# The last row tile of a hybrid attention block: order of three products and the way its normalization is put together

## Chip, cores, metric

One core of a Trainium2 chip runs the whole program. The metric is device time in microseconds (us); lower is better. Engines: TensorE (PE in the profile), VectorE (DVE), ScalarE (ACT), GpSimd (POOL), SyncE (SP).

## The reference

One encoder block for x of 1024 tokens × 1024 channels, float32. Two attention groups (a neighbourhood attention over a 16 × 64 grid and a windowed attention with a sink) give `mixed`, each multiplied by SiLU of its gate. What the change touches is the end:

```
y = mixed @ w_out                       # 1024 x 1024 times 1024 x 1024
x = layer_norm(alpha * x + y) * gain + bias
```

with mean and deviation taken over the 1024 channels of each token.

## The kernel before

Up to about 390 us the kernel projects the input and runs the attention, with an order of work planned in advance (steps, due times and costs per engine). The edit lies behind that, in `final()`, where the order is written out by hand: per engine, instructions run in the order of the lines, and engines wait for one another on semaphores.

**The output product** is done in 2 × 2 blocks with shared partial products in the manner of Strassen, over the first half of the sum, and with plain products over the rest. The loop in `final()` goes over t = 0..3. Pass t finishes two row tiles of 128 tokens: row tile t and row tile 4 + t. Their columns come in two halves of 512: half 0 and half 1. `prod` (L1168) issues the matmuls of one named product, each term three matmuls (high and low float16 parts), 512 columns each. A PSUM bank holds a running sum to which several products are added in turn, and `add` (L1210) lets VectorE add the bank's present content, times a constant, to the row tile `xr` (L1213):

- q1: goes into half 0 of row tile t; in pass 3 its bank is `b[3]`
- q6: added into the same bank; the sum goes into half 1 of row tile t
- q5: its own bank; into half 1 of row tiles t and 4 + t
- q7: added into `b[t]` on top of q6; into half 1 of row tile 4 + t
- d: own bank; half 1 of row tile 4 + t
- p4: added into `b[t]`; half 0 of row tile 4 + t
- q2: half 0 of row tile t (18 matmuls in pass 3)
- q3: half 1 of row tile t; in pass 3 in pieces of 256, 128 and 128 columns

Since q7 is added onto the bank that holds q6, q7 may only start once VectorE has read the bank. With `whole=True` `add` also issues the statistics of the piece (`bn_stats`, L1219; for row tile 3 in pieces of 128). In pass 3 the order on TensorE before the change is q5, q6, q2 (first 6 matmuls), q7, d, p4, q2 (other 12), q3 in three pieces.

**The normalization** of most row tiles is `begin` and `finish`: VectorE puts the statistics together (`bn_aggr`, L1223), ScalarE takes the root (L1225), ScalarE applies scale and shift to the row tile (L1284), GpSimd multiplies by gain and adds bias (L1286, L1287), SyncE sends two transfers of 256 KB (L1288). `norm(7)`, ahead of row tile 3's end, lets VectorE do half of the columns (L1277, L1281).

Row tile 3 comes last. `norm_ahead` (L1238) lets GpSimd multiply its first WP = 256 columns (`HP`) by gain ahead of time. `norm_last` (L1240) then puts bias for these columns into a PSUM bank through the identity (L1243), runs 30 matmuls whose result isn't used (L1246), takes mean (`mv`) and deviation (`sd`), and adds two more matmuls: a diagonal matrix of 1/deviation times x·gain (`dr`, L1251, L1253) and one of -mean/deviation times gain (`dn`, L1252, L1254). ScalarE copies the bank out (L1256). VectorE scales the other columns in two pieces, `H0` (256) and `H1` (512): first (x - mean)·gain (L1248, L1255), then times 1/deviation plus bias (L1258). SyncE sends the two pieces (L1259), ScalarE's queue the first 256 columns (L1260).

Of the kernel before, what the change touches and what calls it, by code (L numbers as in the profile page):

```python
# [7 lines left out]
F32 = mybir.dt.float32  # L8
# [4 lines left out]
AF = mybir.ActivationFunctionType  # L13
ALU = mybir.AluOpType
# [41 lines left out]
WORK = {"act": 0.55, "dve": 0.63, "pool": 1.2}  # L56
STEP = (1.88, 1.5, 1.2)
ROOM = {"act": 0.35, "dve": 0.5, "pool": 0.0}
WP = 256
BWIN = (0, 256, 624, 880)  # L60
VE = HD + 1
ROPE_PERM = list(range(0, 16)) + list(range(32, 48)) + list(range(16, 32)) + list(range(48, 64))
# [3 lines left out]
def hybrid_block(ctx, tc, xT, x, wt, wv, wo, bias, sink, gain, lbias, cos, sin, bmask, out):  # L66
    nc = tc.nc
# [10 lines left out]
    def bank(tag):  # L78
        bufs = {"pj": 2, "s": 4, "t": 2}[tag]
        return (ps1 if bufs == 1 else ps2).tile([128, 512], F32, tag=tag, name=f"ps_{tag}", bufs=bufs)  # L80
# [6 lines left out]
    def big_tile(name, shape=(128, 2, 512), dt=F32R):  # L87
        n = taken[0]
        taken[0] += 1
        tag = "big" if n < 8 or 16 <= n < 24 or n >= 32 + NS else "big2"  # L90
        return big.tile(list(shape), dt, tag=tag, name=name)

    xh, xl, x16h, x16l = {}, {}, {}, {}
    for half in range(2):
        for k in range(KT):
            t = big_tile(f"x{half}{k}", dt=F32 if half else F32R)
# [3 lines left out]
    def zslot(name, tag="z"):  # L100
        return zp.tile([128, S], F32, tag=tag, name=name, bufs=3 if tag == "z" else 1)


    identf = const.tile([128, 128], F32, name="identf")
# [797 lines left out]
    def quad(q):  # L902
        g, p, j, t = units[4 * q]
        return g, p, j, t // 4
# [263 lines left out]
    def prod(name, t, ps, es=None, c=(0, 512)):  # L1168
        o, w = c
        cs = slice(o, o + w)  # L1170
        terms = TERMS[name]
        fresh = name in ("q1", "q2", "q5", "d") or c != (0, 512)
        for e in range(len(terms)) if es is None else es:
            a, b, i = terms[e]
            need(*done.get((a, i), ()), *done.get((b, i), ()))
            (ah, al), (bh, bl) = part[a, i], part[b, i]
            for n, (lh, rh) in enumerate(((ah, bh), (ah, bl), (al, bh))):
                nc.tensor.matmul(ps[:, cs], lh[:, 128 * t:128 * t + 128], rh[:, cs],  # L1178
                                 start=(fresh and e == 0 and n == 0), stop=(e == len(terms) - 1 and n == 2), skip_group_check=True)
                yield  # L1180
# [14 lines left out]
    def final():  # L1195
        actx.close()
        fp = ctx.enter_context(tc.tile_pool(name="fp", bufs=2, reuse_waits="tile"))
# [9 lines left out]
        def x_scale(t):  # L1207
            nc.scalar.activation(xrs[t], xrs[t], AF.Copy, scale=ALPHA)

        def add(t, a, ps, c=(0, 512), whole=False):  # L1210
            o, w = c
            xv = xrs[t][:, 512 * a + o:512 * a + o + w]
            nc.vector.scalar_tensor_tensor(xv, ps[:, o:o + w], yc, xv, op0=ALU.mult, op1=ALU.add)  # L1213
            if whole:
                if t not in stats:
                    stats[t] = fp.tile([128, 8, 6], F32, name=f"stats{t}", bufs=1)
                b = 128 if t == 3 else 512
                for i in range(w // b):
                    nc.vector.bn_stats(stats[t][:, (512 * a + o) // b + i, :], xv[:, b * i:b * i + b])  # L1219

        def row_stats(t):
            mv = fp.tile([128, 2], F32, tag="mv", name="mv")
            nc.vector.bn_aggr(mv, stats[t][:, :8 if t == 3 else 2, :])  # L1223
            sd = fp.tile([128, 1], F32, tag="sd", name="sd")
            nc.scalar.activation(sd, mv[:, 1:2], AF.Sqrt, bias=eps)  # L1225
            return mv, sd

        def row_scale(mv, sd, on_dve=True):
            rstd = fp.tile([128, 1], F32, tag="rstd", name="rstd")
            nc.vector.reciprocal(rstd, sd)  # L1230
            nmr = fp.tile([128, 1], F32, tag="nmr", name="nmr")
            (nc.vector if on_dve else nc.gpsimd).tensor_scalar(nmr, mv[:, 0:1], rstd, -1.0, op0=ALU.mult, op1=ALU.mult)  # L1232
            return rstd, nmr

        HP, H0, H1 = slice(0, WP), slice(WP, WP + 256), slice(WP + 256, 1024)

        def norm_ahead(t):
            nc.gpsimd.tensor_mul(xrs[t][:, HP], xrs[t][:, HP], gb[:, HP])  # L1238

        def norm_last(t):  # L1240
            ts = slice(128 * t, 128 * t + 128)
            xr = xrs[t]
            nc.tensor.matmul(pn[:, :WP], identf, bb[:, HP], start=True, stop=False)  # L1243
            busy = bank("s")
            for _ in range(30):
                nc.tensor.matmul(busy[:, :128], warm, warm, start=True, stop=True)  # L1246
            mv, sd = row_stats(t)
            nc.vector.scalar_tensor_tensor(xr[:, H0], xr[:, H0], mv[:, 0:1], gb[:, H0], op0=ALU.subtract, op1=ALU.mult)  # L1248
            rstd, nmr = row_scale(mv, sd)
            dr, dn = (fp.tile([128, 128], F32, name=n, bufs=1) for n in ("dr", "dn"))  # L1250
            nc.scalar.activation(dr, identf, AF.Copy, scale=rstd)  # L1251
            nc.scalar.activation(dn, identf, AF.Copy, scale=nmr)  # L1252
            nc.tensor.matmul(pn[:, :WP], dr, xr[:, HP], start=False, stop=False)  # L1253
            nc.tensor.matmul(pn[:, :WP], dn, gb[:, HP], start=False, stop=True)  # L1254
            nc.vector.scalar_tensor_tensor(xr[:, H1], xr[:, H1], mv[:, 0:1], gb[:, H1], op0=ALU.subtract, op1=ALU.mult)  # L1255
            nc.scalar.copy(xr[:, HP], pn[:, :WP])  # L1256
            for h in (H0, H1):
                nc.vector.scalar_tensor_tensor(xr[:, h], xr[:, h], rstd, bb[:, h], op0=ALU.mult, op1=ALU.add)  # L1258
                nc.sync.dma_start(out[ts, h], xr[:, h])  # L1259
            nc.scalar.dma_start(out[ts, HP], xr[:, HP])  # L1260
# [3 lines left out]
        def begin(t):  # L1264
            begun.append((t, *row_stats(t)))

        def finish():
            while begun:
                norm(*begun.pop())
# [23 lines left out]
        a, b = ([obank.get((name, t)) for t in range(4)] for name in ("q2", "q1"))  # L1293
        add(0, 0, b[0])
        m_last()
        gb, bb = zslot("gb"), zslot("bb")
# [8 lines left out]
        def run(name, t, ps, *args):  # L1305
            list(prod(name, t, ps, *args))
            return ps

        c01 = [run("q5", t, bank("t")) for t in range(2)]
        for t in range(4):  # L1310
            cb = c01[t] if t < 2 else run("q5", t, bank("s"))
            if t == 0:
                run("q2", 0, a[0], (5,))
                add(0, 0, a[0], whole=True)
                run("q2", 1, a[1], (5,))
            run("q6", t, b[t])
            if t > 0:
                add(4 + t, 1, cb)
            add(t, 1, b[t])
            if t == 3:  # L1320
                add(t, 1, cb)
            finish()
            if t == 0:
                add(4, 1, cb)
                add(1, 0, b[1])
                add(1, 0, a[1], whole=True)
            if t == 1:
                add(2, 0, b[2])
                run("q2", 2, a[2], (5,))
                add(2, 0, a[2], whole=True)  # L1330
            for n in ((5, 2), (6, 3), (7,), ())[t]:
                x_scale(n)
            if t < 3:
                d = run("d", t, bank("pj"))
                run("q7", t, b[t])
            else:
                a[3] = run("q2", 3, bank("pj"), (0, 1))
                run("q7", t, b[t])
                add(7, 1, b[3])
                d = run("d", t, bank("pj"))  # L1340
            add(4 + t, 1, d, whole=t == 3)
            if t < 3:
                add(4 + t, 1, b[t], whole=True)
            if t == 2:
                b[3] = run("q1", 3, bank("s"))
                add(3, 0, b[3])
            if t < 3:
                run("q3", t, cb)
                add(t, 1, cb, whole=True)
                begin(t)  # L1350
            run("p4", t, b[t])
            add(4 + t, 0, b[t], whole=True)
            if t == 3:
                norm(7)
            else:
                finish()
                begin(4 + t)
        add(3, 0, run("q2", 3, a[3], range(2, 6)), whole=True)
        norm_ahead(3)
        cuts = [((0, 256), bank("t")), ((256, 128), None), ((384, 128), None)]  # L1360
        pn = bank("t")
        for c, ps in cuts:
            ps = ps or bank("pj" if c[0] == 256 else "s")
            add(3, 1, run("q3", 3, ps, None, c), c, whole=True)
        norm_last(3)

    def m_last():
# [14 lines left out]
    for i in range(-LD, NU + LO):  # L1382
# [5 lines left out]
        per, h = divmod(i, 16)  # L1388
# [3 lines left out]
        if i in SCAN_LD:  # L1392
            n, b = divmod(NSCAN + SCAN_LD.index(i), 4)
# [9 lines left out]
        if i in B_LD:  # L1403
            n = B_LD.index(i)
# [50 lines left out]
        if 0 <= q < NU // 4:  # L1455
            g, p, j, h = quad(q)
# [93 lines left out]
```

## Time and profile before

| | |
|---|---|
| median of 3 runs | 442.7 us (443.14, 442.70, 441.31) |
| the profiled execution | 441.67 us |
| its span in the trace | 439.9 us |
| TensorE busy | 433.5 us (99%) |
| VectorE, ScalarE, GpSimd busy | 335.0, 314.2, 279.4 us |
| granted TensorE clock | 0.999 |

The execution is the device's time for the run; the span is what the trace covers, from the first instruction to the last. Starts in the rows are us from the beginning of the span. A group `128x512 f32<-128x512 f32 x2` gives partitions × elements of output and input, and the count. In merged rows the length runs to the modelled end of the last matmul, so neighbouring TensorE rows overlap a little.

### The profile page before, as it was taken

Reading aid. Unit: us, or ns where it says so; the run is one execution under the profiler, and the core shown is the slowest. Engines: PE = TensorE matmul, PEld = TensorE weight load, DVE = VectorE, ACT = ScalarE, POOL = GpSimd, SP = SyncE. Lnnn points to the kernel's source line nnn. Section 1 sums busy time; section 2 is a strip of 40 time slices with the busy share of each in tenths; the row PEclk is TensorE's granted clock in tenths of the full one; section 3 lists DMA queues with packets and bytes.
Section 4 is the critical chain, followed back from the end, with each engine's and each line's share of the span. In section 5 each row is a group of like instructions: output and inputs, shape, how many; then the busy total and the mean of one; then the engine's idle time right before and its main releaser. Section 6 shows DMA issues by size and latency. Waiting matters only on the chain.

```text
span 439.9 us, 9401 instructions
## 1 busy us (share of the span) xinstructions
PE 433.5 (99%) x3235; PEld 253.7 (58%) x3235; DVE 335.0 (76%) x820; ACT 314.2 (71%) x662; POOL 279.4 (64%) x299
## 2 busy tenths in 40 slices
PE   9999999999999999999999999999999999999995
PEld 8997754444445555565555565655556555444454
DVE  5978967775978798889788977878778855575556
ACT  5849789767698889798988979788788763341221
POOL 0110074577439558779998799797989871067683
PEclk9999999999999999999999999999999999999999
DMA  8922569995329998996859999989799959711113
GB/s 273 406 82 60 140 235 332 260 302 166 101 67 196 187 192 172 212 165 122 194 106 214 218 210 195 221 184 181 147 203 214 169 114 372 288 48 75 70 73 120
DMA packets 128815, 80.12 MB, mean 182 GB/s; under 512 B 97280, under 2 KB 106368, under 8 KB 128768
## 3 DMA queue, kind: packets, MB, share of 16 engines
q1 hardware_dynamic: 128624, 79.40, 73.9%
q8 instruction: 25, 0.41, 0.4%
q14 instruction: 22, 0.18, 0.1%
q10 hardware_dynamic: 144, 0.13, 0.1%
HBM read 48.01 MB, written 8.42 MB: 128 GB/s over the span
## 4 chain that ended last, share of the span: by engine, by line
PE 97%; DVE 2%; ACT 0%; issue 0%; DVEq 0%; ACTq 0%
PE ps_pj L430 49%; PE ps_s L1178 9%; PE ps_t L925 7%; PE ps_s L537 6%; PE ps_pj L1178 4%; PE ps_s L860 4%; PE ps_s L861 4%; PE ps_pj L537 3%; PE ps_t L537 3%; PE ps_t L1178 2%; PE ps_t L948 2%; PE ps_t L463 1%; DVE stats L1219 1%; DVE xr L1213 1%; DVE xr L1281 0%
## 5 line engine op out<-in xcount | busy, mean ns | idle before, releaser
L430 PE MATMUL ps_pj<-xf,wh 128*128 128x512 f16 x672 | 201.5, 379 | 0.0
L430 PE MATMUL ps_pj<-xf,wl 128*128 128x512 f16 x336 | 127.5, 379 | 0.0
L430 PEld LDWEIGHTS <-wh 128*128 128x128 f16 x672 | 63.7, 98 | 59.8
L885 ACT ACTIVATE ps_s<-sn,nm 128x385 f32<-128x385 f32 (+3 forms) x128 | 71.0, 554 | 30.2 <-DVE nm L870 29.7
L896 DVE SCALAR_TENSOR_TENSOR split<-ps_s,split 128x384 f16<-128x384 f32 (+1 forms) x128 | 66.8, 522 | 17.8 <-ACT split L895 16.3
L245 POOL TENSOR_SCALAR wr<-wr,wsc 128x512 f32<-128x512 f32 x32 | 22.9, 717 | 65.2 <-ACT wh L240 59.9
L895 ACT ACTIVATE split<-ps_s 128x384 f16<-128x384 f32 (+1 forms) x128 | 58.1, 454 | 1.6
L430 PEld LDWEIGHTS <-wl 128*128 128x128 f16 x336 | 32.9, 98 | 38.1
L870 DVE CUSTOM_DVE_ANT_0 sn<-ps_s,bias,sg 128x368 f32<-128x368 f32 (+1 forms) x64 | 36.2, 566 | 13.8 <-PE ps_s L861 13.2
L870 DVE CUSTOM_DVE_ANT_0 sn<-ps_s,bm,nsk 128x384 f32<-128x384 f32 (+1 forms) x64 | 40.8, 638 | 6.5 <-PE ps_s L861 6.1
L246 POOL TENSOR_TENSOR wl<-wr,wh 128x512 f16<-128x512 f32 x32 | 40.3, 1261 | 2.7
L860 PE MATMUL ps_s<-ks,qs 128*128 128x384 f16 (+2 forms) x128 | 39.7, 310 | 0.0
L861 PE MATMUL ps_s<-ks,qs 128*128 128x384 f16 (+2 forms) x128 | 39.7, 310 | 0.0
L925 PEld LDWEIGHTS <-tr 128*128 128x128 f16 (+1 forms) x1056 | 36.3, 98 | 2.4
L1178 PEld LDWEIGHTS <-A 128*128 128x128 f16 x216 | 20.2, 98 | 20.7
L347 POOL COPY ks<-ks 64x512 f16<-64x512 f16 x40 | 25.9, 647 | 4.6 <-ACT ks L298 2.0
L1213 DVE SCALAR_TENSOR_TENSOR xr<-ps_s,yc,xr 128x512 f32<-128x512 f32 (+1 forms) x22 | 16.0, 727 | 14.8 <-PE ps_s L1178 14.0
L1284 ACT ACTIVATE xr<-xr,nmr,rstd 128x1024 f32<-128x1024 f32 x6 | 7.4, 1240 | 27.0 <-POOL nmr L1232 27.0
L1178 PEld LDWEIGHTS <-m 128*128 128x128 f16 x144 | 13.9, 98 | 15.8
L537 PEld LDWEIGHTS <-xf 128*128 128x128 f16 x192 | 18.6, 98 | 7.2
L240 ACT ACTIVATE wh<-wr,wsc 128x512 f16<-128x512 f32 x32 | 22.7, 710 | 0.0
L1286 POOL TENSOR_TENSOR xr<-xr,gb 128x512 f32<-128x512 f32 x13 | 16.8, 1291 | 8.3 <-ACT xr L1284 8.1
(216 smaller groups left out, 897.7 us busy)
## 6 DMA issues: line engine op xcount, KB each, us to landing
wr<-in_wt SPq DMA_DIRECT2D x32, 256.0 KB, 3.6
ws<-in_wt SPq DMA_DIRECT2D x15, 512.0 KB, 6.8
wor<-in_wo SPq DMA_DIRECT2D x20, 256.0 KB, 3.7
xr<-in_x SPq DMA_DIRECT2D x8, 512.0 KB, 10.5
out<-xr SPq DMA_DIRECT2D x15, 256.0 KB, 2.0
wob<-in_wo SPq DMA_DIRECT2D x14, 256.0 KB, 3.8
bias<-in_bias SPq DMA_DIRECT2D x8, 440.0 KB, 4.5
wvraw<-in_wv SPq DMA_DIRECT2D x9, 320.0 KB, 5.3
```

What stands on the lines that cost most here:

```text
L246: nc.gpsimd.tensor_sub(l, raw, h)
L347: nc.gpsimd.tensor_copy(place(t, o, half, col), place(t, a, half, col))
L430: nc.tensor.matmul(ps, a[:, k % 4, :], mv, start=(k == 0 and i == 0), stop=(k == KT - 1 and i == 2))
L537: nc.tensor.matmul(ps[:, :320], lh[:, ts], rh[:, cs], start=(k == ko[0] and i == 0), stop=(k == ko[-1] and i == 2))
L860: nc.tensor.matmul(ps[:, :n], q, sl[0], start=True, stop=False)
L861: nc.tensor.matmul(ps[:, :n], q, sl[1], start=False, stop=True)
L870: nc.vector.tensor_tensor_reduce(sn[:, :n], ps[:, :n], bias_t, sg[:, c:c + 1], init, op0=ALU.add, op1=ALU.min, accum_out=nm)
L885: nc.scalar.activation(pt[:, :m], sn[:, :m], AF.Exp, bias=nm, scale=-1.0, accum_out=acc)
L895: nc.scalar.activation(hl[:, :m, 0, :], src, AF.Copy, scale=PSCALE)
L896: nc.vector.scalar_tensor_tensor(hl[:, :m, 1, :], src, PSCALE, hl[:, :m, 0, :], op0=ALU.mult, op1=ALU.subtract)
L925: nc.tensor.matmul(ps[:, w * m:w * m + e], a, b_, start=(i == 0), stop=(i == len(mms) - 1))
L1178: nc.tensor.matmul(ps[:, cs], lh[:, 128 * t:128 * t + 128], rh[:, cs], start=(fresh and e == 0 and n == 0), stop=(e == len(terms) - 1 and ...
```

## The change

Three things, all in the last pass and behind it:

1. In pass 3 the order becomes q6, q5, q7, d, p4, q2 (all 18 matmuls in one go), q3. q6's sum is read by VectorE's first add, then come the two adds of q5.
2. WP becomes 384: the first 384 columns of row tile 3 go through the bank, `H0` is columns 384 to 640 and `H1` columns 640 to 1024 (384 of them).
3. In `norm_last` the bank gets three matmuls: the identity times x·gain, a diagonal matrix `dm` of -mean (made by GpSimd) times gain, and a diagonal matrix `ds` of the deviation (made by ScalarE) times bias. ScalarE multiplies by 1/deviation while it copies the bank out. The unused matmuls become 20 and stand ahead of the identity's matmul. `H1` is scaled and sent ahead of `H0`.

```
-WP = 256
+WP = 384
...
-            nc.tensor.matmul(pn[:, :WP], identf, bb[:, HP], start=True, stop=False)
             busy = bank("s")
-            for _ in range(30):
+            for _ in range(20):
                 nc.tensor.matmul(busy[:, :128], warm, warm, start=True, stop=True)
+            nc.tensor.matmul(pn[:, :WP], identf, xr[:, HP], start=True, stop=False)
             mv, sd = row_stats(t)
+            rstd = fp.tile([128, 1], F32, tag="rstd", name="rstd")
+            dm, ds = (fp.tile([128, 128], F32, name=n, bufs=1) for n in ("dm", "ds"))
+            nc.gpsimd.tensor_scalar(dm, identf, mv[:, 0:1], -1.0, op0=ALU.mult, op1=ALU.mult)
+            nc.scalar.activation(ds, identf, AF.Copy, scale=sd)
+            nc.tensor.matmul(pn[:, :WP], dm, gb[:, HP], start=False, stop=False)
+            nc.tensor.matmul(pn[:, :WP], ds, bb[:, HP], start=False, stop=True)
+            nc.vector.scalar_tensor_tensor(xr[:, H1], xr[:, H1], mv[:, 0:1], gb[:, H1], op0=ALU.subtract, op1=ALU.mult)
+            nc.vector.reciprocal(rstd, sd)
             nc.vector.scalar_tensor_tensor(xr[:, H0], xr[:, H0], mv[:, 0:1], gb[:, H0], op0=ALU.subtract, op1=ALU.mult)
-            rstd, nmr = row_scale(mv, sd)
-            dr, dn = (fp.tile([128, 128], F32, name=n, bufs=1) for n in ("dr", "dn"))
-            nc.scalar.activation(dr, identf, AF.Copy, scale=rstd)
-            nc.scalar.activation(dn, identf, AF.Copy, scale=nmr)
-            nc.tensor.matmul(pn[:, :WP], dr, xr[:, HP], start=False, stop=False)
-            nc.tensor.matmul(pn[:, :WP], dn, gb[:, HP], start=False, stop=True)
-            nc.vector.scalar_tensor_tensor(xr[:, H1], xr[:, H1], mv[:, 0:1], gb[:, H1], op0=ALU.subtract, op1=ALU.mult)
-            nc.scalar.copy(xr[:, HP], pn[:, :WP])
-            for h in (H0, H1):
+            nc.scalar.activation(xr[:, HP], pn[:, :WP], AF.Copy, scale=rstd)
+            for h in (H1, H0):
                 nc.vector.scalar_tensor_tensor(xr[:, h], xr[:, h], rstd, bb[:, h], op0=ALU.mult, op1=ALU.add)
                 nc.sync.dma_start(out[ts, h], xr[:, h])
             nc.scalar.dma_start(out[ts, HP], xr[:, HP])
...
         for t in range(4):
-            cb = c01[t] if t < 2 else run("q5", t, bank("s"))
+            cb = c01[t] if t < 2 else run("q5", t, bank("s")) if t == 2 else None
...
             run("q6", t, b[t])
+            if t == 3:
+                add(t, 1, b[t])
+                cb = run("q5", t, bank("s"))
             if t > 0:
                 add(4 + t, 1, cb)
-            add(t, 1, b[t])
-            if t == 3:
-                add(t, 1, cb)
+            add(t, 1, cb if t == 3 else b[t])
             finish()
...
             else:
-                a[3] = run("q2", 3, bank("pj"), (0, 1))
                 run("q7", t, b[t])
...
-        add(3, 0, run("q2", 3, a[3], range(2, 6)), whole=True)
+        add(3, 0, run("q2", 3, bank("pj")), whole=True)
```

## The prediction

> **What bounds the kernel now.** I read the page first, then the chain of work that ended last, then the timelines of the last 25 us by engine. The page:
>
> ```profile
> span 439.9 us, 9401 instructions
> ```
> ```profile
> PE 97%; DVE 2%; ACT 0%; issue 0%; DVEq 0%; ACTq 0%
> ```
>
> TensorE carries 97% of the chain. The edit starts at the loop pass t = 3, so only the end of the program can move. There the chain of waits changes engine:
>
> ```profile
> 420.80 3.90 PE ps_s L1178 x18
> 424.70 0.02 issue
> 424.72 0.76 DVE xr L1213
> ```
>
> Columns: start, length, what. The 18 matmuls are p4 of pass 3. From their end the chain runs on VectorE, while TensorE still has the rest of q2 and q3 to do. TensorE's timeline (start, busy):
>
> ```profile
> 412.86 2.75 PE L1178 MATMUL ps_s<-T,m 128*128 128x512 f16 x12
> 415.45 1.46 PE L1178 MATMUL ps_pj<-wo,m 128*128 128x512 f16 x6
> 416.75 1.46 PE L1178 MATMUL ps_s<-T,m 128*128 128x512 f16 x6
> ```
> ```profile
> 424.52 2.75 PE L1178 MATMUL ps_pj<-wo,A 128*128 128x512 f16 x12
> ```
> ```profile
> 431.08 0.65 PE L1243 MATMUL ps_t<-bb,identf 128*128 128x256 f32 x2
> ```
>
> 412.86 is q5 and q6, 415.45 the first third of q2 (its group starts 1.30 before the next), 416.75 is q7, 424.52 the rest of q2. The last product ends where L1243 starts, 431.08. VectorE's timeline shows when its result is taken:
>
> ```profile
> 432.13 0.33 DVE L1213 SCALAR_TENSOR_TENSOR xr<-ps_s,yc,xr 128x128 f32<-128x128 f32 x1
> ```
>
> The last add starts at 432.13, about 0.85 after a product ready by 431.28 (431.08 and the 0.20 that lies between q2's start at 424.52 and the add of p4 at 424.72). So VectorE's backlog sets the end, and it starts with p4. The last part of the chain:
>
> ```profile
> 432.90 0.38 DVE mv L1223
> ...
> 433.32 0.32 issue
> 433.64 0.30 ACT sd L1225
> ...
> 434.16 0.41 ACT dr L1251
> 434.57 0.14 issue
> ...
> 435.90 0.37 ACT xr L1256
> ```
>
> and the transfers behind it (timeline, then DMA issues with KB and time to landing):
>
> ```profile
> 436.31 0.37 ACTq L1260 DMA_DIRECT2D out<-xr  x1
> ```
> ```profile
> out<-xr SPq DMA_DIRECT2D x1, 256.0 KB, 2.1
> out<-xr SPq DMA_DIRECT2D x1, 128.0 KB, 1.8
> out<-xr ACTq DMA_DIRECT2D x1, 128.0 KB, 2.3
> ```
>
> ScalarE's transfer lands at 436.31 + 2.3 = 438.61. The remaining 439.90 - 438.61 = 1.29 is the program's end, which I leave as it is.
>
> **The change, part by part. The order of products (q6, q5, q7; q2 whole behind p4).** The matmuls are the same ones. Six of q2 leave the place ahead of q7, so p4 may end 1.30 earlier. But q6 and q7 write one bank, and q7 must wait until VectorE has read q6's sum. The adds:
>
> ```profile
> 414.78 0.75 DVE L1213 SCALAR_TENSOR_TENSOR xr<-ps_s,yc,xr 128x512 f32<-128x512 f32 x1
> ```
> ```profile
> 415.65 0.75 DVE L1213 SCALAR_TENSOR_TENSOR xr<-ps_s,yc,xr 128x512 f32<-128x512 f32 x1
> ```
>
> Before, the second of these reads q6, ends at 416.40, and q2's six matmuls cover it. After, q6 is done by about 414.36 (412.86 + 1.30 + 0.20), its add is the first and ends at 414.78 + 0.75 = 415.53; q5 covers TensorE only to 415.45. With a hand-over of 0.14 (the issue row between dr and L1253) q7 starts at 415.67: a **wait of 0.22** that did not exist. Behind q7 on TensorE stand all later products, and for them VectorE's adds; each waits with it. Bounds: 0, if the add runs earlier in VectorE's queue, and 1.9, if the add of q5 stays ahead: that starts at 415.65 for its last matmul, the q6 add follows to 417.2, and q7 starts at 417.33. I take 0.22, from the order of the diff.
>
> So p4 ends 1.30 - 0.22 = 1.08 earlier and its add starts at 423.64. All products end 0.22 later, at 431.30. The backlog from p4's add to the last add took 432.13 - 424.72 = 7.41 us; from 423.64 it would be through at 431.05. The last product is there only at 431.50, so TensorE is late next, and the last add goes from 432.13 to **431.50: -0.63**. mv, done at 433.28 before, is done at 432.65. Cutting q2 in one piece costs nothing itself: it needs a bank that q5 or d left long before, and TensorE is never without work up to q3.
>
> **The normalization.** Before, from mv on: sd, rstd, dr, two matmul pairs, copy. After: bias and mean go in unscaled; x·gain through the identity, -mean·gain through dm, deviation·bias through ds, and the way out multiplies by rstd. rstd leaves the path to the matmuls; nmr and dn go; ten idle matmuls go (they fill TensorE while it waits, now for GpSimd; thirty would hold it 0.6 longer). What comes: 384 columns instead of 256 in every piece, and dm on GpSimd. GpSimd and VectorE have to be read side by side:
>
> ```profile
> 425.68 1.26 POOL L1286 TENSOR_TENSOR xr<-xr,gb 128x512 f32<-128x512 f32 x1
> 427.02 1.60 POOL L1287 TENSOR_TENSOR xr<-xr,bb 128x512 f32<-128x512 f32 x1
> 428.74 1.56 POOL L1286 TENSOR_TENSOR xr<-xr,gb 128x512 f32<-128x512 f32 x1
> 430.38 1.27 POOL L1287 TENSOR_TENSOR xr<-xr,bb 128x512 f32<-128x512 f32 x1
> 431.61 0.73 POOL L1238 TENSOR_TENSOR xr<-xr,gb 128x256 f32<-128x256 f32 x1
> ```
> ```profile
> 426.55 0.94 DVE L1277 SCALAR_TENSOR_TENSOR xr<-xr,mv,gb 128x512 f32<-128x512 f32 x1
> ```
> ```profile
> 427.73 1.44 DVE L1281 SCALAR_TENSOR_TENSOR xr<-xr,rstd,bb 128x512 f32<-128x512 f32 x1
> ```
> ```profile
> 433.30 0.48 DVE L1248 SCALAR_TENSOR_TENSOR xr<-xr,mv,gb 128x256 f32<-128x256 f32 x1
> 434.30 0.74 DVE L1255 SCALAR_TENSOR_TENSOR xr<-xr,mv,gb 128x512 f32<-128x512 f32 x1
> ```
>
> L1255 with GpSimd idle takes 0.74. L1281, the same form, takes 1.44 and ends 0.55 after GpSimd's operation does (428.62 to 429.17); L1277 ends 0.55 after 426.94. In turn the GpSimd operations that start inside them grow from 1.27 to 1.60 and 1.56. They take turns.
>
> The Trainium skill, "SBUF — State Buffer", section "SBUF: two separate sides", says the same more sharply: a VectorE operation with two SBUF inputs and a GpSimd operation that reads SBUF exclude each other for the whole instruction. By that rule dm, issued just after VectorE's first scaling, starts only when that ends; the trace agrees (1.44 against 0.74). Plain sharing would let dm finish at 433.1, and the last matmuls would end at 435.28 instead of 435.47 below.
>
> Step by step. GpSimd's own queue ahead of it was already full, and VectorE's L1277 and L1281 come 1.08 earlier but still fall into it, two turns as before: x·gain starts at 431.61 before, about 431.7 after, and 384 columns are priced between 0.73 (256) and 1.27 (512) at 1.00: done at 432.7. The identity pair starts at 432.70 + 0.14 = 432.84; TensorE is through its 20 idle matmuls by then (30 took 1.84, so 431.30 + 1.23 = 432.53). The spacing of one pair is 435.22 - 434.71 = 0.51 for 256 columns by the timeline:
>
> ```profile
> 434.71 0.67 PE L1253 MATMUL ps_t<-xr,dr 128*128 128x256 f32 x2 [1.30 <-ACT dr L1251]
> 435.22 0.60 PE L1254 MATMUL ps_t<-gb,dn 128*128 128x256 f32 x2
> ```
>
> so 0.77 for 384, and this pair is through at 433.6. VectorE's scaling of 384 columns (0.61, between 0.48 and 0.74) runs from 432.67 to 433.28, then dm:
>
> ```profile
> L245 POOL TENSOR_SCALAR wr<-wr,wsc 128x512 f32<-128x512 f32 x32 | 22.9, 717 | 65.2 <-ACT wh L240 59.9
> ```
> ```profile
> 414.71 0.27 POOL L1232 TENSOR_SCALAR nmr<-mv,rstd 128x1 f32<-128x1 f32 x1 [1.96 <-DVE rstd L1230]
> ```
>
> between 0.27 (1 column) and 0.72 (512): 0.38 by line, done at 433.66, pair at 433.80. ds: 432.65 + 0.36 + 0.30 for sd, then 0.41 as dr took, is 433.74, inside the dm pair, so free; it would bind only 0.7 later. The ds pair starts at 433.80 + 0.77 = 434.57 and takes 0.60 × 1.5 = 0.90: 435.47. Way out:
>
> ```profile
> L394 ACT ACTIVATE z<-ps_pj,invt 128x512 f32<-128x512 f32 x10 | 6.8, 679 | 4.6 <-PE ps_pj L430 4.6
> ```
>
> 0.37 (256 columns, a copy) to 0.68 (512, scaled per row as here) bound it; 0.57, nearer the scaled row. It starts 0.08 after the matmuls (before, 435.82 to 435.90) and ends at 436.12; the transfer is issued 0.04 later, at **436.16, against 436.31: -0.15**. rstd, wanted only there, is made on VectorE right after sd at 433.31, two us ahead; from there rstd and three pieces (0.48, 0.61, 0.48) end near 435.1, so SyncE's two transfers, now in the other order, are issued at about 434.6 and 435.1, off the path; no other queue is passed. So of the 0.63, 0.48 is given back by dm's turn and the wider bank.
>
> Landing of 192 KB: 1.8 and 2.1 are SyncE's rows for 128 and 256 KB, 2.3 is ScalarE's while 256 KB were under way; SyncE's are now an issue second ahead. I take 2.1, bounds 1.9 and 2.5: 438.26 against 438.61. **Sum: -0.35.** The span becomes 439.55 and the execution 441.67 - 0.35 = 441.3. That execution stands 1.03 below the median of the three runs; I carry the difference over: 442.7 - 0.35, given as **442.3**.
>
> **The rivals.** *Faster:* no wait at q7 and no turn-taking at dm; the last add at 431.28, and GpSimd's x·gain alone orders the pairs: last matmul 435.28, transfer 435.97, landing 1.95: -0.7, 442.0. For it: q6 is done 0.4 before its add starts. Against: L1281's 1.44.
>
> *Slower: the wait at q7.* If the q6 add is second in VectorE's queue, q7 waits 1.9. Then products end at 432.98, the last add starts at 433.18, mv is done at 434.33 (1.68 later than in the forecast), all that follows shifts with it, and the sum is -0.35 + 1.68 = +1.3: 444.0. It turns at a wait of 0.22 + 0.35 = 0.6, that is q7 starting after 416.0. Against: the add's operands are there at 414.36.
>
> *Nothing gained:* the engines' order stays as before although the lines moved, and only the normalization changes: mv at 433.28, dm 434.29, pairs to 436.10, transfer 436.79, landing 2.1: +0.3, 443.0. A sum near it, +0.1, comes if GpSimd's 384 columns end at 433.36, after two more turns of 0.33 (1.60 - 1.27). For it: dm's turn costs most just there.
>
> **How the numbers follow.** Forecast 0.55, faster 0.13, nothing gained 0.15, slower 0.07, and 0.10 for a cause that no row shows (code order upstream). No listed case leaves 0.5% (2.2 us), about what a measurement of this kernel can tell from no change. The three runs lie 1.8 apart, which carries about 4 in 100 of each sign over the bound from these cases; the unseen cause adds 5 and 4. Faster 0.09, same 0.83, slower 0.08. The range takes the cases (442.0 to 444.0) with half the scatter (0.9) below and, as 444.0 is rare, to 443.6 above; the low end is 440.9.
>
> **What would show it.** q7's first matmul 1.1 earlier than 416.75, after a gap of about 0.2; p4's add 1.1 earlier; the last add waiting for TensorE; dm ending about 0.4 after VectorE's first scaling; the last transfer 0.1 to 0.4 earlier. A gap over 0.6 ahead of q7, an idle TensorE inside q2 or q3, or another time before 412.86 would prove me wrong.

## The result, and the profile after

| | before | changed kernel |
|---|---|---|
| median, 22 runs each | 442.16 us | 441.13 us |
| range | 441.31 to 444.15 | 440.38 to 442.82 |
| span of the profiled execution | 439.9 us | 439.3 us |

The ratio is 0.9977, with a 95% interval of 0.9967 to 0.9987: 1.0 us faster, 0.6 to 1.5. The forecast was -0.35 us, from the same mechanism.

The two spans can't be compared directly. The first matmul of the q5/q6 pair of pass 3 starts at 412.86 before and at 413.37 after, although no line ahead of it was changed; over all profiles of this case, one per kernel and all with the same lines ahead of it, it starts between 412.80 and 414.52. So all that follows is **counted from the start of this pair**. In that count ScalarE's last transfer is issued at 436.31 - 412.86 = 23.45 before and 436.21 - 413.37 = 22.84 after, and lands at 25.75 and 24.74: 1.01 us earlier, as much as the measured gain. The issue in the changed kernel, from the timeline:

```profile
436.21 0.37 ACTq L1261 DMA_DIRECT2D out<-xr  x1
```

TensorE's timeline of the changed kernel:

```profile
413.37 4.12 PE L1178 MATMUL ps_s<-T,m 128*128 128x512 f16 x18
417.32 0.38 PE L1178 MATMUL ps_pj<-z,A 128*128 128x512 f16 x1
```

q6, q5 and q7 are one unbroken row of 18 matmuls. From its start to the next product, d, are 3.95 us; 18 such matmuls (q5, q6 and six of q2) took 416.75 - 412.86 = 3.89 before. So the wait at q7 is about 0.06 us. It is the hand-over from VectorE's add of q6 to q7's first matmul (all engines' timeline; PEld rows are TensorE's weight loads):

```profile
415.28 0.70 DVE L1213 SCALAR_TENSOR_TENSOR xr<-ps_s,yc,xr 128x512 f32<-128x512 f32 x1
...
416.03 0.96 PEld L1178 LDWEIGHTS <-m 128*128 128x128 f16 x5 [0.19 <-issue]
```

The add ends at 415.98. The weights of q7's first matmul were loaded ahead of that; the load at 416.03 is that of its second, which begins when the first matmul runs. VectorE's timeline further on:

```profile
424.00 0.75 DVE L1213 SCALAR_TENSOR_TENSOR xr<-ps_s,yc,xr 128x512 f32<-128x512 f32 x1 [2.40 <-PE ps_s L1178]
...
431.86 0.35 DVE L1213 SCALAR_TENSOR_TENSOR xr<-ps_s,yc,xr 128x128 f32<-128x128 f32 x1 [0.33 <-PE ps_s L1178]
432.25 0.29 DVE L1219 BATCH_NORM_STATS2 stats<-xr 128x6 f32<-128x128 f32 x1
432.64 0.37 DVE L1223 BATCH_NORM_AGGREGATE mv<-stats 128x2 f32<-128x48 f32 x1
433.05 0.62 DVE L1254 SCALAR_TENSOR_TENSOR xr<-xr,mv,gb 128x384 f32<-128x384 f32 x1
433.71 0.16 DVE L1255 RECIPROCAL rstd<-sd 128x1 f32<-128x1 f32 x1
433.79 0.47 DVE L1256 SCALAR_TENSOR_TENSOR xr<-xr,mv,gb 128x256 f32<-128x256 f32 x1
```

The brackets give the idle time ahead of an instruction and what ended it. p4's add comes at 10.63 in place of 11.86, the last add at 18.49 in place of 19.27, and ahead of the last add VectorE now stands idle for 0.33 until TensorE has the last product. VectorE's backlog is gone. The end of the chain of waits:

```profile
430.89 1.27 POOL xr L1288
432.16 0.96 POOL xr L1238
433.12 0.04 issue
433.17 0.91 PE ps_t L1246 x2
434.08 0.79 PE ps_t L1252 x2
434.87 0.66 PE ps_t L1253 x2
435.53 0.03 ACTq L1257
435.56 0.04 issue
435.60 0.58 ACT xr L1257
```

It no longer runs through VectorE. GpSimd's x·gain (L1238) releases the identity's pair, and the three pairs follow without a gap. GpSimd's timeline and the DMA issues:

```profile
432.12 0.99 POOL L1238 TENSOR_TENSOR xr<-xr,gb 128x384 f32<-128x384 f32 x1
433.11 0.79 POOL L1250 TENSOR_SCALAR dm<-identf,mv 128x128 f32<-128x128 f32 x1
```
```profile
out<-xr SPq DMA_DIRECT2D x1, 192.0 KB, 1.9
out<-xr ACTq DMA_DIRECT2D x1, 192.0 KB, 1.9
out<-xr SPq DMA_DIRECT2D x1, 128.0 KB, 1.8
```

dm takes 0.79 beside VectorE's first scaling and ends at 433.90, 0.23 after the scaling does. ScalarE's 192 KB land in 1.9 us, where its 128 KB took 2.3.

### The profile page after: what moved, and what is told of

Read it like the earlier page. It is cut to its first block, busy times and chain, and to the rows that moved or that the text cites. A ratio compares the mean times of both kernels' runs of the same rounds, so it can differ in the third digit from the quotient of the medians.

```text
span 439.3 us, 9382 instructions
## 1 busy us (share of the span) xinstructions
PE 434.3 (99%) x3225; PEld 253.6 (58%) x3225; DVE 334.9 (76%) x819; ACT 314.1 (72%) x661; POOL 280.4 (64%) x300
## 4 chain that ended last, share of the span: by engine, by line
PE 94%; POOL 3%; ACT 1%; DVE 0%; issue 0%; POOLq 0%; ACTq 0%
PE ps_pj L430 50%; PE ps_s L1178 8%; PE ps_t L925 7%; PE ps_s L537 6%; PE ps_s L860 4%; PE ps_s L861 4%; PE ps_pj L1178 4%; PE ps_pj L537 3%; PE ps_t L537 3%; PE ps_t L1178 2%; PE ps_t L948 2%; POOL xr L1287 2%; POOL xr L1288 2%; PE ps_t L463 1%; ACT xr L1285 1%; POOL xr L1238 0%
## 5 line engine op out<-in xcount | busy, mean ns | idle before, releaser
L1285 ACT ACTIVATE xr<-xr,nmr,rstd 128x1024 f32<-128x1024 f32 x6 | 7.4, 1240 | 27.0 <-POOL nmr L1232 27.0
```

## The experiments

Theory A: the order of products takes away VectorE's backlog, which is worth about 0.8 us by itself; the normalization adds a little. Theory B: what VectorE wins is taken back by GpSimd's queue, and the gain is in the normalization and its transfers. All times from the start of the pair:

| kernel | last add | ScalarE's transfer issued | last landing | ratio to before (95%) |
|---|---|---|---|---|
| before | 19.27 | 23.45 | 25.75 | 1 |
| changed | 18.49 | 22.84 | 24.74 | 0.9977 (0.9967 to 0.9987) |
| order_only | 18.49 | 22.68 | 24.98 | 0.9981 (0.9967 to 0.9994) |
| norm_only | 19.28 | 23.62 | 25.52 | 0.9995 (0.9982 to 1.0008) |
| q6_second | 20.08 | 24.43 | 26.33 | 1.0013 (1.0001 to 1.0025) |
| narrow_bank | 18.49 | 22.45 | 24.55 | 0.9971 (0.9958 to 0.9984) |
| narrow_dm_vector | 18.49 | 22.09 | 24.7 (SyncE's) | 0.9975 (0.9960 to 0.9991) |
| narrow_dm_vector_awake | 18.49 | 21.81 | 24.6 (SyncE's) | 0.9981 (0.9962 to 1.0000) |

"Last landing" adds the time to landing in the DMA issues, which has one decimal, to the time of issue; it is read from one traced execution of each kernel, and the span ends 1.2 to 1.3 us behind it in all of them. Each ratio is to executions of the kernel before taken in the same series: their median is 442.16 us for the changed kernel, 442.14 for the four kernels below it and 442.68 for the last two. In the four, the last landing moves against before by -0.77, -0.23, +0.58 and -1.20; by the ratios it is -0.84, -0.22, +0.57 and -1.28 us. So what happens behind the pair's start is enough to explain the times.

**order_only.** The new order with the normalization of before, so the changed kernel less its `norm_last`:

```
-WP = 384
+WP = 256
...
-            nc.tensor.matmul(pn[:, :WP], dm, gb[:, HP], start=False, stop=False)
-            nc.tensor.matmul(pn[:, :WP], ds, bb[:, HP], start=False, stop=True)
+            nc.tensor.matmul(pn[:, :WP], dr, xr[:, HP], start=False, stop=False)
+            nc.tensor.matmul(pn[:, :WP], dn, gb[:, HP], start=False, stop=True)
```

> The new order of products with the old normalization (WP = 256, 1/deviation in the diagonal matrices). Times are counted from the first matmul of the q5/q6 pair of pass 3; there the last add starts at 19.27 in the kernel before and 18.49 in the changed one, ScalarE's transfer is issued at 23.45 and 22.84. Theory A (the order takes away VectorE's backlog, and that is worth 0.8 us by itself): last add at 18.5, transfer issued at 22.7, landing 2.3 us later as before, since SyncE's 256 KB are still just ahead of it; 0.8 us faster than before, ratio 0.998. Theory B (the order gives VectorE time that GpSimd's queue takes back; the gain is in the normalization and its transfers): the last add also at 18.5, but the transfer at 23.3 or later, ratio 0.9995 to 1.000.

```profile
433.25 0.48 DVE L1248 SCALAR_TENSOR_TENSOR xr<-xr,mv,gb 128x256 f32<-128x256 f32 x1
```
```profile
436.26 0.37 ACTq L1260 DMA_DIRECT2D out<-xr  x1
```

The first scaling, from VectorE's timeline, and ScalarE's issue, with the pair at 413.58: the scaling at 19.67 (20.44 before), the issue at 22.68, and the landing still 2.3. That is 0.77 earlier than before, and the ratio is 0.9981: theory A, in its numbers. Theory B's 23.3 falls.

**norm_only.** The old order with the new `norm_last` and WP = 384; against the changed kernel:

```
-                cb = run("q5", t, bank("s"))
...
+                a[3] = run("q2", 3, bank("pj"), (0, 1))
...
-        add(3, 0, run("q2", 3, bank("pj")), whole=True)
+        add(3, 0, run("q2", 3, a[3], range(2, 6)), whole=True)
```

> The old order of products with the new normalization (WP = 384). Theory A: the last add stays at 19.3 and mv at 20.4; VectorE's first scaling holds dm up until 21.05, dm ends 0.23 later, two matmul pairs and the way out put the transfer at 23.6, 0.1 later than before; it lands 1.9 us after its issue in place of 2.3; together 0.3 us faster, ratio 0.9993. Theory B: the new normalization shortens the path from mv to the transfer by 0.6 us and the landing by 0.4: ratio 0.998.

```profile
434.94 0.62 DVE L1254 SCALAR_TENSOR_TENSOR xr<-xr,mv,gb 128x384 f32<-128x384 f32 x1
```
```profile
435.00 0.79 POOL L1250 TENSOR_SCALAR dm<-identf,mv 128x128 f32<-128x128 f32 x1 [0.77 <-DVE mv L1223]
```
```profile
435.85 0.91 PE L1252 MATMUL ps_t<-gb,dm 128*128 128x384 f32 x2 [0.65 <-POOL dm L1250]
```

VectorE, GpSimd and TensorE around dm, with the pair at 414.48. Here mv is late and TensorE has been through the identity's pair for 0.65 us when dm comes, so dm's turn is on the path. The transfer is issued 0.17 later than before, and lands 0.4 sooner after its issue: -0.23 together. The ratio's interval reaches over 1, so only the trace shows it. The two parts, -0.77 and -0.23, add up to -1.00, against -1.01 for the whole.

**q6_second.** The changed kernel with one pair of adds exchanged:

```
             if t == 3:
-                add(t, 1, b[t])
                 cb = run("q5", t, bank("s"))
             if t > 0:
                 add(4 + t, 1, cb)
+            if t == 3:
+                add(t, 1, b[t])
```

> The changed kernel with one pair of adds swapped: VectorE adds q5 to row tile 7 ahead of reading q6's sum. Theory A (q7 waits for VectorE's reading of the bank, every us of this wait moves the end by a us): q7 starts at 4.3 instead of 2.7 after the pair's start, a gap of 1.6 us on TensorE, the last add at 20.1, the transfer at 24.4; 1.6 us slower than the changed kernel, 0.6 slower than before: ratio to before 1.0014. Rival (the slack ahead of the last add, or GpSimd's queue, takes the wait up): within 0.3 us of the changed kernel, ratio 0.998.

```profile
414.26 2.75 PE L1178 MATMUL ps_s<-T,m 128*128 128x512 f16 x12
418.51 1.46 PE L1178 MATMUL ps_s<-T,m 128*128 128x512 f16 x6 [1.50 <-DVE xr L1213]
```

TensorE stands 1.50 us ahead of q7 and VectorE's add ends it. Every later step moves with it: the landing is 1.59 later than in the changed kernel, and a gain of 1.0 becomes a loss of 0.6 by the order of two adds.

**narrow_bank.** The changed kernel with one number undone:

```
-WP = 384
+WP = 256
```

> The changed kernel with WP = 256 in place of 384: 256 columns go through the bank, VectorE's first piece is 512 columns. Theory A (the wider bank costs: three pairs and the way out are on the path): GpSimd's x times gain ends 0.26 earlier, pairs are 0.51 apart instead of 0.77, VectorE's longer first piece holds dm 0.12 longer; transfer issued at 22.4 instead of 22.84, 0.3 to 0.4 us faster than the changed kernel unless the 256 KB of SyncE make the landing 2.3 again; ratio to before 0.9965 to 0.9975. Rival (the narrower pieces of VectorE pay for the change): the 512 columns bring VectorE and SyncE's transfer back onto the path; same as the changed kernel or up to 0.3 slower, ratio 0.998.

```profile
432.31 0.70 PE L1246 MATMUL ps_t<-xr,identf 128*128 128x256 f32 x2
433.52 0.70 PE L1252 MATMUL ps_t<-gb,dm 128*128 128x256 f32 x2 [0.52 <-DMA out<-xr]
```
```profile
432.48 0.75 DVE L1254 SCALAR_TENSOR_TENSOR xr<-xr,mv,gb 128x512 f32<-128x512 f32 x1
```
```profile
432.55 0.93 POOL L1250 TENSOR_SCALAR dm<-identf,mv 128x128 f32<-128x128 f32 x1 [0.29 <-DVE mv L1223]
```

The transfer is issued at 22.45, as theory A said, and lands 2.1 later: 0.19 ahead of the changed kernel in the trace. The two ratios, 0.9971 and 0.9977, can't be told apart. So no run shows a gain from the wider bank. TensorE now waits 0.52 for dm (the releaser named is a DMA; by time it is dm, which ends at 433.48), and dm ends 0.25 after VectorE's 0.75 of scaling does.

**narrow_rstd_first** (one execution only). The same with VectorE's reciprocal ahead of its first scaling, so that VectorE stands idle while dm is made:

```
+            nc.vector.reciprocal(rstd, sd)
             nc.vector.scalar_tensor_tensor(xr[:, H1], xr[:, H1], mv[:, 0:1], gb[:, H1], op0=ALU.subtract, op1=ALU.mult)
-            nc.vector.reciprocal(rstd, sd)
```

> The changed kernel with WP = 256 and VectorE's reciprocal placed ahead of its first scaling, so that VectorE stands idle from mv until the root is there, and GpSimd makes dm in that time. Theory (GpSimd and VectorE take turns): dm takes 0.35 to 0.4 us in place of 0.93, its pair starts 0.55 to 0.6 after mv in place of 1.08. Rival (dm takes that long by itself): dm stays at 0.8 to 0.9. The end is not the point: VectorE's pieces come 0.9 later and SyncE's last transfer sets it, 0.1 to 0.3 us slower than the narrow bank alone.

```profile
434.26 0.37 POOL L1250 TENSOR_SCALAR dm<-identf,mv 128x128 f32<-128x128 f32 x1 [0.27 <-DVE mv L1223]
```

Alone, dm takes 0.37 in place of 0.93, and its pair starts 0.53 after mv in place of 1.08. The run ends later, as SyncE's last piece is issued only some 0.6 after ScalarE's: the last landing is 0.5 later than in narrow_bank, where 0.1 to 0.3 had been expected. The turn-taking is shown. The Trainium skill, "SBUF — State Buffer", section "SBUF: two separate sides", says that GpSimd and a VectorE operation with two SBUF inputs hold one port pair in turn for whole instructions; these three durations of one instruction (0.37 alone, 0.79 behind 0.62, 0.93 behind 0.75) agree with it. But dm ends only 0.23 to 0.25 after VectorE's scaling, less than the 0.37 that it takes alone, so some of its time passes while VectorE still works.

**narrow_dm_vector.** WP = 256 and the diagonal of the mean made by VectorE:

```
-            nc.gpsimd.tensor_scalar(dm, identf, mv[:, 0:1], -1.0, op0=ALU.mult, op1=ALU.mult)
+            nc.vector.tensor_scalar(dm, identf, mv[:, 0:1], -1.0, op0=ALU.mult, op1=ALU.mult)
```

> The changed kernel with WP = 256 and the diagonal of the mean made by VectorE, ahead of its first scaling, in place of GpSimd. Theory (with the narrow bank dm's turn behind VectorE's 512 columns holds the path): dm's pair starts right behind the identity's, at 20.1 from the pair's start in place of 20.7, the pair of ds at 20.8 in place of 21.3, the transfer at 22.0 in place of 22.45; SyncE's transfers move 0.2 later to 21.85 and 22.3, landing 2.1 to 2.3; 0.2 to 0.45 us faster than the narrow bank alone, ratio to before 0.996 to 0.9967. Rival (VectorE's queue takes it back: every piece of VectorE is later by dm, and SyncE's last transfer then ends the run): no faster than the narrow bank, ratio 0.997.

```profile
432.84 0.29 DVE L1250 TENSOR_SCALAR dm<-identf,mv 128x128 f32<-128x128 f32 x1
```
```profile
out<-xr SPq DMA_DIRECT2D x1, 256.0 KB, 2.1
out<-xr ACTq DMA_DIRECT2D x1, 128.0 KB, 2.2
out<-xr SPq DMA_DIRECT2D x1, 128.0 KB, 2.5
```

ScalarE's transfer goes out at 22.09, 0.36 earlier than in narrow_bank, but the last landing is at 24.7 in place of 24.55, and the ratios 0.9975 and 0.9971 can't be told apart: the rival. All 512 KB are now issued within half a microsecond, and SyncE's 128 KB, issued at 435.36 with the pair at 413.16, land last, 2.5 us later.

**narrow_dm_vector_awake.** The same, with a one-column copy on ScalarE ahead of the root:

```
+            awake = fp.tile([128, 1], F32, name="awake", bufs=1)
+            nc.scalar.copy(awake, stats[t][:, 6, 0:1])
             mv, sd = row_stats(t)
```

> The same, and ScalarE does a one-column copy (of a statistics column, result not used) when the statistics of the last piece but one are there, about 1 us ahead of the root. In all kernels ScalarE starts the root 0.36 to 0.38 us after mv when it was idle for 5 us, and 0.10 after it when it was idle for 3.6 us or less. Theory (the delay comes from the long idle time): root 0.1 after mv, ds and its pair 0.26 earlier, the transfer at 21.7; 0 to 0.2 us faster than without it. Rival (the delay belongs to this instruction, for instance to where its code lies): the root stays 0.36 behind mv, no change.

```profile
431.14 0.19 ACT L1248 COPY awake<-stats 128x1 f32<-128x1 f32 x1 [3.62 <-DVE stats L1219]
432.68 0.29 ACT L1225 ACTIVATE sd<-mv,eps 128x1 f32<-128x1 f32 x1 [1.35 <-DVE mv L1223]
```

mv is done at 432.21 + 0.37 = 432.58, so the root starts 0.10 after it; without the copy it was 0.37 to 0.39. The transfer is issued 0.28 earlier still, and again SyncE's landing ends the run; the ratio can't be told from that without the copy. So a copy 1.35 us ahead takes the delay away. That the length of the idle time makes the delay is not shown, for other rows speak against it. In the changed kernel's timeline:

```profile
422.00 0.26 POOL L1232 TENSOR_SCALAR nmr<-mv,rstd 128x1 f32<-128x1 f32 x1
422.30 1.24 ACT L1285 ACTIVATE xr<-xr,nmr,rstd 128x1024 f32<-128x1024 f32 x1 [5.36 <-POOL nmr L1232]
```
```profile
433.39 0.29 ACT L1225 ACTIVATE sd<-mv,eps 128x1 f32<-128x1 f32 x1 [5.43 <-DVE mv L1223]
```

After 5.36 us of idle time L1285 starts 0.04 after GpSimd's nmr; after 5.43 the last root starts 0.38 after VectorE's mv (432.64 + 0.37 = 433.01).

**order_no_big_send** (one execution only). order_only, but SyncE's 256 KB of the last row tile go out early, with the gain in place of the result in those columns:

```
-                nc.sync.dma_start(out[ts, h], xr[:, h])
+                if h is H0:
+                    nc.sync.dma_start(out[ts, h], xr[:, h])
...
         norm_ahead(3)
+        nc.sync.dma_start(out[384:512, H1], gb[:, H1])
```

> The new order with the old normalization, but SyncE's 256 KB of row tile 3 are not sent at the end: in their place the same number of bytes of the gain tile goes out some 5 us earlier, so those columns of the output hold the gain. Theory (the landing of ScalarE's transfer is long because SyncE's 256 KB are under way): transfer issued at 22.7 from the pair's start as before, landing 1.8 to 1.9 us later in place of 2.3. Rival (2.3 belongs to ScalarE's queue and to 1 KB per partition): landing stays at 2.3.

```profile
out<-xr SPq DMA_DIRECT2D x1, 128.0 KB, 1.8
out<-xr ACTq DMA_DIRECT2D x1, 128.0 KB, 1.8
```

The transfer is issued at 22.68 as in order_only and lands in 1.8 in place of 2.3. The long landing came from the 256 KB under way beside it.

## Why the prediction was right, and where it was too small

The direction and the mechanism were right, and so was TensorE as the engine that the last add waits for; the size was a third of the measured one. That 441.13 lies inside the range is in part luck: the fastest case listed was 442.0, and only the 0.9 of scatter put below it takes the range past the measurement. By its own sum that end is 442.0 - 0.9 = 441.1, not the 440.9 given; 441.13 lies inside by either. By its own steps:

- **The wait at q7** (forecast 0.22): 0.06. VectorE's add of q6 took 0.70, not 0.75, and the hand-over from VectorE to TensorE about 0.05, not the 0.14 borrowed from a ScalarE row (dr to L1253); GpSimd's, from L1238 to L1246, was 0.05 too, and so was ScalarE's own from ds to TensorE in narrow_dm_vector_awake (433.41 to 433.46).
- **p4's add** (1.08 earlier): 1.23. **The last add** (0.63 earlier, waiting for TensorE): 0.78, with the 0.33 of idle time to show it. Both differences, 0.15, come from the 0.16 of the step above.
- **What the normalization gives back** (forecast 0.48): 0.61 was left of the 0.78, so 0.17. This is the term that was furthest off, by 0.31. The single prices held: x·gain 0.99 (forecast 1.00), scaling 0.62 (0.61), way out 0.58 (0.57). But dm ended 0.23 behind VectorE's scaling, not 0.38, and both hand-overs were shorter, so dm was done at 433.90, inside the identity's pair (433.17 + 0.79 = 433.96). Its turn, which the forecast had on the path, cost at most 0.04 here (the next pair took 0.75 to the start of the last), and the chain of waits runs through GpSimd's x·gain instead. So dm's pair started 0.95 after mv, where the forecast had 1.15, which is 0.20 of the 0.31. The last pair took 0.81, not 0.90, which is 0.09 more.
- **The landing** (forecast 2.1): 1.9. The reason given, SyncE's pieces about a microsecond ahead, is what order_no_big_send shows. The change takes 0.4 here, where the forecast had 0.2.
- **The sum**: -1.0 in place of -0.35. The rest of the distance between 442.3 and 441.13 is the base: 442.7 was the median of three runs, and the median of 22 was 442.16. With 22 runs each, a change of 0.23% could be told from none; the forecast had put that limit at about 0.5%.

Of the rivals, "slower" is the mechanism of q6_second: the forecast put it 1.68 above its own end, and measured were 1.59 above the changed kernel. "Nothing gained" put the normalization alone at +0.3; norm_only shows -0.23, by the same two terms. "Faster" came closest (-0.7), though one of its two conditions, no turn-taking at dm, did not hold: the turn was there and was covered. Its other condition, no wait at q7, nearly did, and x·gain orders the pairs as it said.

The prediction also named another time before 412.86 as a sign of being wrong, and the pair did start at 413.37. It starts at 412.80 in narrow_bank, which has the same lines ahead of it, so this is read here as scatter between executions. Not settled is why the pair's start differs by up to 1.7 us with the same work ahead of it; no kernel was traced twice.

## What to carry to other kernels

When an engine falls behind near the end, look for the point where its backlog begins and bring that work's input forward, even if another engine's total stays the same: here 0.8 us came from moving six matmuls behind p4. Here the move put a read of a shared bank next to the next write, and the order of the reader's queue then decided between gain and loss. Where several last transfers went out within half a microsecond, an earlier issue of one of them bought nothing that the runs show. Where SyncE's pieces went out a microsecond ahead, ScalarE's landed sooner, so it is worth trying to spread them.

## What the runs showed of the hardware

- ScalarE started the last root 0.37 to 0.39 us after its input when it had been idle for 5 us, and 0.10 after it with a tiny copy 1.35 us ahead. Another of its instructions started 0.04 after its input when it had been idle for 5.36 us, so idle time alone doesn't make the delay. What does, no run shows.
- One GpSimd instruction of 128x128 took 0.37 us with VectorE idle, and 0.79 or 0.93 when it started just behind a VectorE scaling of 0.62 or 0.75; it then ended 0.23 to 0.25 after the scaling.
- A transfer of 128 KB took 1.8, 2.3 or 2.5 us to land: 2.3 with 256 KB issued 0.2 ahead on the other queue, 1.8 without them, and 2.5 as the last of 512 KB issued within half a microsecond.
